# Pooling input and merge gates as seven half products, with their sums and other operands made in earlier stages

## The chip, the cores and the metric

The kernel runs on one core of one Trainium2 chip. The metric is device time in microseconds (us). A core has a matrix engine (TensorE, called PE in the profile), a vector engine (VectorE, DVE), an activation engine (ScalarE, ACT), a general engine (GpSimd, POOL) and a sync engine (SyncE, SP) that here only issues transfers. Each engine works through its own queue of instructions in order and waits on semaphores for the others. Matrices are read by PE from on-chip memory (SBUF), and its results stand in eight PSUM banks of 128 x 512 float32.

## The reference

One layer of an encoder, for 1024 tokens of width 1024, float32 throughout:

```python
h = rmsnorm(x, norm_mix)
q, k, v, r, lr_f, lr_b, u, g_a, g_b = split(h @ w_in)    # widths 512 512 1024 1024 16 16 512 1024 1024
o = gla(q, k, v, decay(lr_f)) + flip(gla(flip ..., decay(lr_b)))   # 4 heads, forward and backward scan
o = per_head_rmsnorm(o) * gla_norm * silu(r)
y_a = o @ w_branch_gla
pooled = window_mean(u, 2 / 4 / 8 / 16 per channel group) - u
y_b = (pooled @ w_pool_group) * pool_scale
x = x + (sigmoid(g_a) * y_a + sigmoid(g_b) * y_b) @ w_out
gate, up = split(rmsnorm(x, norm_ffn) @ w_ffn_in)         # 2 x 2816 columns
x = x + (silu(gate) * up) @ w_ffn_out
out = rmsnorm(x, norm_final)
```

What the change touches is the projection of h to u, g_a and g_b (2560 of the columns of w_in), and where the operands of `y_a` and of the product with w_out are prepared.

## The kernel before

Every operand of a large product is split into two float32r parts: `hi` is the value cast, `lo` the value less `hi`. A product a b is made of three matmuls, hi hi, hi lo and lo hi (`products`, L250); `mm3` issues the three for one 128 x 128 block of the left side and 512 columns of the right. `split_to` (L172 and L173) makes the parts: a cast on ScalarE, then a subtraction on POOL for weights and mostly on DVE for the rest.

*Seven products for eight.* In the branch product, the merged product and both FFN products, left and right matrix are cut into 2 x 2 blocks and the result is made of seven block products of sums and differences (numbered 1 to 7 in the code) instead of eight (a Strassen-Winograd scheme). Such a product of blocks is called a half product. Such sums are extra vector work. All projections out of `w_in` (q, k, v, r, u, g_a, g_b) are done plainly.

*Weights.* `load` (L180) issues transfers from SP into a ring of four raw buffers; `order` lists which columns of `w_in` come when; `take` hands out the next weights and `prepare` puts the split of the ones after them into the list `pending`. `pump`, called after each `mm3`, releases one pending split each time two `mm3` of 512 columns have been issued.

*Work beside.* The order on each engine is written out by hand, without a scheduler. Vector work that accompanies matmuls is written as generators. `begin` puts one in the list `side`, and `pump` resumes the first of them when as many `mm3` have been issued as its last `yield` said. `finish_side` runs them out at once. `attention` (L450 on) is such a generator: decay factors, the backward scan, the scores, the forward scan, for one head, beside the projections of the next head. In the scan each step (`advance`) goes from PE (`kv`) to DVE (`st`, L539) to ScalarE (`sf`, L615) and back to PE (`op`, L616).

*Stages*, by the time in the trace: normalization and transposes, with v of head 0 and the low-rank decay (to about 74 us); q, k, v of heads 1 to 3 with the attention of the head before beside each (74 to 284); r with the rest of the last attention, where o is transposed and multiplied by silu(r) into `oT` (284 to 394, L655 to L675); the gate stage (394 to 633, L948 to L995); the branch product (633 to 709); the merged product with w_out (709 to 794); the FFN-in product, 22 `Unit`s of seven products (794 to 1225); the FFN-out product (1225 to 1451).

*The gate stage before.* For each of the four groups g there is one 128-column block of u, and two blocks each of g_a and g_b, each block being 2 halves x 8 `mm3`. u goes through `pooled` (a generator: running window sums on DVE), its result stays in SBUF and is multiplied with the group's weights into `yb`; the gates go through a sigmoid, g_b's is multiplied by yb, and both go to DRAM (`sa_out`, `yb_out`). After each half, `beside` (L941) resumes one step of preparations for later stages: `branch_sums` (sums of blocks of w_branch on POOL, L753), `output_parts` (sums of blocks of w_out on POOL, L778, then their split, all stored to `wo_out`), `unit_parts` (the operands of the first two FFN units, stored to `u_out`). `later` notes a store, and `flush` (L685 to L690) issues those noted, on ScalarE's queue. `early` makes three sets of sums of oT for the branch product at the end of the stage (L865, L867, L870).

SBUF is used in 39 slots of 512 KB (128 partitions x 1024 float32) beside smaller rings.

```python
    def later(dst, src):
        deferred.append(partial(nc.scalar.dma_start, dst, src))
...
            for half in range(2):
                ps = feature_major(wa, hT, half)
                nc.scalar.activation(sa[:, half, :], ps[:, :], AF.Sigmoid)
                beside(j)
            flush()
            later(sa_out[:, :, j, :], sa[:, :, :])
```

Of the kernel before, what the change touches and what calls it, by code (L numbers as in the profile page):

```python
# [42 lines left out]
AHEAD = 4  # L43

# [5 lines left out]
def kernel(  # L50
# [91 lines left out]
    side = []  # L142
# [3 lines left out]
    def pump(dt):  # L146
        if pending:
            credit[0] += dt
            if credit[0] >= 2:
                credit[0] = 0.0  # L150
                pending.pop(0)()
        if not side:
            return
        side[0][1] -= dt
        while side and side[0][1] <= 0:
            try:
                side[0][1] += next(side[0][0])
            except StopIteration:
                side.pop(0)
# [55 lines left out]
    for g in range(GROUPS):  # L215
        order.append((w_in, KT, U0 + g * P, P))
        for j in (2 * g, 2 * g + 1):
            order.append((w_in, KT, GA0 + j * P, P))
            if j == 2 * g:
                order.append((w_pool_group[0, g], 1, 0, 2 * P))  # L220
            order.append((w_in, KT, GB0 + j * P, P))
# [214 lines left out]

    v_heads, o_heads, unscaled = {}, {}, []
# [11 lines left out]
    def attention(h, q, k):  # L449
# [181 lines left out]
        o_heads[h] = o  # L631

        def normalize():
            for n in range(NT):
                t = o[n // 4][:, n % 4, :]
                nc.vector.tensor_scalar(t, t, rs[:, n : n + 1], None, op0=ALU.mult)

# [3 lines left out]

    for h in range(HEADS):
# [11 lines left out]
    oT = {}  # L654
    for j in range(KT):  # L655
        if j == 6:
            finish_side()
        if j % 4 == 0:
            for half in range(2):
                oT[j // 4, half] = [slot(s="o") for _ in range(2)]  # L660
        w = take()
        for half in range(2):
# [4 lines left out]
            for i in range(4):  # L667
# [5 lines left out]
                oT[j // 4, half][j % 4 // 2][:, j % 2, :], tp[:, :], g_gla[:, j : j + 1], sr[:, :],  # L673
                op0=ALU.mult, op1=ALU.mult,
            )  # L675


    sa_out, yb_out = (dram.tile([P, 2, KT, HALF], F32, name=n) for n in ("sa_out", "yb_out"))
    deferred = []

    def later(dst, src):
        deferred.append(partial(nc.scalar.dma_start, dst, src))

    def flush():
        while deferred:  # L685
            deferred.pop(0)()

# [28 lines left out]

    add = partial(nc.vector.tensor_tensor, op=ALU.add)
    sub = partial(nc.vector.tensor_tensor, op=ALU.subtract)
    psub = partial(nc.gpsimd.tensor_tensor, op=ALU.subtract)
    padd = partial(nc.gpsimd.tensor_tensor, op=ALU.add)

    s_out = {p: dram.tile([P, 4, HALF], F32, name=f"s_out{p}") for p in (3, 5, 6, 7)}
    wo_out = {p: dram.tile([2, P, 4, HALF], F32, name=f"wo_out{p}") for p in range(1, 8)}
    READY = 2
    f_order = [f for q in range(PAIRS) for f in (q, q + PAIRS)]
    u_out = [{p: dram.tile([P, 2, HALF], F32, name=f"u_out{n}_{p}") for p in range(1, 8)} for n in range(READY)]

    def chunk(w, k_half, c_half, c):
        k0 = (4 * k_half + 2 * c) * P
        return w[k0 : k0 + 2 * P, c_half * HALF : (c_half + 1) * HALF].rearrange("(k p) c -> p k c", p=P)  # L740

    def branch_sums(c):
        raw = {}
        for i in range(2):
            for j in range(2):
                raw[i, j] = slot(s="wsum")
                nc.sync.dma_start(raw[i, j][:, :, :], chunk(w_branch, j, i, c))
        yield
        x11, x12, x21, x22 = (raw[i, j][:, :, :] for i in range(2) for j in range(2))
        for op, dst, a, b, p in (  # L750
            (padd, x22, x21, x22, 5), (psub, x21, x11, x21, 7), (psub, x11, x22, x11, 6), (psub, x12, x12, x11, 3)
        ):
            op(dst, a, b)  # L753
            later(s_out[p][:, 2 * c : 2 * c + 2, :], dst)
            if p in (7, 3):
                yield
        yield

    def output_parts(c):
        raw = {}  # L760
        for i in range(2):
            for j in range(2):
                raw[i, j] = slot(s="wsum")
                nc.sync.dma_start(raw[i, j][:, :, :], chunk(w_out, i, j, c))
        yield
        b11, b12, b21, b22 = (raw[i, j][:, :, :] for i in range(2) for j in range(2))

        def parts(p, src):
            hi, lo = slot(F32R, s="wph"), slot(F32R, s="wpl")
            split_to(hi[:, :, :], lo[:, :, :], src)  # L770
            for n, t in enumerate((hi, lo)):
                later(wo_out[p][n][:, 2 * c : 2 * c + 2, :], as_f32(t[:, :, :]))

        for p, src, dst, a, b in (
            (1, b11, b11, b12, b11), (3, b22, b12, b22, b12), (7, b12, b22, b22, b11), (2, b21, b21, b21, b22)
        ):
            parts(p, src)
            psub(dst, a, b)  # L778
            if p in (3, 2):
                yield  # L780
        for p, src in ((5, b11), (6, b22), (4, b21)):
            parts(p, src)
            if p != 5:
                yield
        yield

    def unit_parts(n):
        raw = []
        for c0 in (f_order[n] * P, D_FF + f_order[n] * P):
            raw.append(slot(F32, (KT, P), "fraw"))  # L790
            nc.sync.dma_start(raw[-1][:, :, :], w_ffn_in[:, c0 : c0 + P].rearrange("(k p) c -> p k c", p=P))
        yield
        a11, a12, a21, a22 = (t[:, 4 * j : 4 * j + 4, :].rearrange("p k c -> p (k c)") for t in raw for j in range(2))

        def parts(p, src):
            both = slot(F32R, s="up")
            split_to(both[:, 0, :], both[:, 1, :], src)
            later(u_out[n][p][:, :, :], as_f32(both[:, :, :]))

        parts(1, a11)  # L800
        parts(4, a22)
        padd(a22, a21, a22)
        psub(a21, a11, a21)
        yield
        parts(2, a12)
        parts(5, a22)
        psub(a11, a22, a11)
        psub(a12, a12, a11)
        yield
        for p, src in ((7, a21), (6, a11), (3, a12)):  # L810
            parts(p, src)
        yield
        yield
# [43 lines left out]
    ob = {(i, j): oT[i, 1 - j] for i in range(2) for j in range(2)}  # L857
    t2s = []
    begun = {}

    def branch_sum(p, c):

        b11, b12, b21, b22 = (ob[i, j][c][:, :, :] for i in range(2) for j in range(2))
        if p == 5:
            sub(b11, b12, b11)  # L865
        elif p == 7:
            sub(b12, b22, b12)  # L867
        elif p == 6:
            t2s.append(slot(s="t2"))
# [4 lines left out]
    def branch_piece(p, c):  # L874
# [6 lines left out]
        def sums():  # L881
            if p == 4:
                branch_sum(4, c)

        def make(raw):
            b = {1: ob[0, 0], 2: ob[1, 0], 3: ob[1, 1], 4: ob[1, 0], 5: ob[0, 0], 6: t2s, 7: ob[0, 1]}[p][c]
            return weight_split(raw), begun.pop((p, c), None) or data_split(b)
# [46 lines left out]
    preps = [g for c in range(2) for g in (branch_sums(c),)] + [output_parts(c) for c in range(2)]  # L934
    preps = chain(*preps, *(unit_parts(n) for n in range(READY)))

    def begin_first(c):
        begun[1, c] = data_split(ob[0, 0][c])

    early = [partial(begin_first, c) for c in range(2)]  # L940
    early += [partial(branch_sum, p, c) for p in (5, 7, 6) for c in range(2)]  # L941

    def beside(j):
        next(preps, None)
        if j == KT - 1:
            for _ in range(2):
                early.pop(0)()

    for g in range(GROUPS):
        w = take()  # L950
        u = [t2(HALF + 2 * PAD, s="u") for _ in range(2)]
        nc.gpsimd.memset(u[0][:, :PAD], 0.0)
        nc.gpsimd.memset(u[1][:, PAD + HALF :], 0.0)
        for half in range(2):
            ps = feature_major(w, hT, half)
            nc.scalar.copy(u[half][:, PAD : PAD + HALF], ps[:, :])
        pool = slot(F32R, s="ph"), slot(F32R, s="pl")
        begin(pooled(g, u, *pool), 1)
        for j in (2 * g, 2 * g + 1):
            c = slice((j % 2) * P, (j % 2 + 1) * P)  # L960
            wa = take()
            if j == 2 * g:
                wp = take()(0)
            sa = slot(s="sa")
            for half in range(2):
                ps = feature_major(wa, hT, half)
                nc.scalar.activation(sa[:, half, :], ps[:, :], AF.Sigmoid)
                beside(j)
            flush()
# [659 lines left out]
```

## Time and profile before

| what | before |
| --- | --- |
| median of 3 runs | 1452.88 us (1450.63 to 1453.42) |
| the profiled execution's own time | 1452.8 us |
| its span in the profile | 1451.1 us |
| mean granted clock of TensorE | 0.995 |
| PE busy | 1405.5 us, 97%, 6797 instructions |
| DVE busy | 872.5 us, 60% |
| POOL busy | 743.8 us, 51% |
| ACT busy | 561.8 us, 39% |
| moved by DMA | 234.15 MB |

The span runs from the first to the last instruction in the profile, and the execution's own time is 1.7 us longer. A row of the table by stage gives the window and its length, then busy time and count of instructions of each engine, the granted clock, the share of time in which the 16 DMA engines are busy, and GB/s. A row of the timeline gives the start, the duration, the engine, the line of the kernel, the operation and its tiles, and in brackets how long the engine stood idle before it and what released it. A row of the groups gives the line, engine, operation and shapes with the count, then busy time in us with the mean in ns, then the idle time before and what ended it. Matmuls overlap in the pipeline, so a matmul's own duration is longer than the distance to the next.

### The profile page before, as it was taken

The page shows a single profiled execution, that of the slowest core. Times are in us where ns is not written, and L with a number is a line of the kernel's source. Part 1 is how long each engine was busy: PE and PEld are TensorE (multiplying, and loading weights), DVE is VectorE, ACT ScalarE, POOL GpSimd, SP SyncE. Part 2 cuts the span into 40 slices and gives each one's busy share as a digit, 9 for nine tenths or more (in the row PEclk, how much of TensorE's full clock was granted, in tenths as well). Part 3 has the DMA queues.
Part 4 walks back from the last instruction along what each step waited for, and adds up shares of the span by engine and source line. Part 5 has one row for each costly group of instructions (what it writes and reads, how often), then busy time and mean ns, then how long its engine had stood idle before and what let it go on. Part 6 is the DMA issues. An engine that isn't in the chain of part 4 may idle for free. (4 is left out here: it accounts for less than half of the span.)

```text
span 1451.1 us, 18652 instructions
## 1 busy us (share of the span) xinstructions
PE 1405.5 (97%) x6797; PEld 1179.6 (81%) x6797; DVE 872.5 (60%) x1111; ACT 561.8 (39%) x995; POOL 743.8 (51%) x510
## 2 busy tenths in 40 slices
PE   7999999999999999999999989999999999999988
PEld 6889898888888787888777778888888888778876
DVE  6266767662132463477994777777677777465375
ACT  6364655652122333344125523322323323444243
POOL 3240413222264553456743457666666668597355
PEclk9999999999999999999999999999999999999999
DMA  6120201011176768686666556444544446966362
GB/s 186 44 58 2 59 16 44 15 30 37 50 224 206 274 214 293 236 290 252 191 203 225 182 178 195 152 154 160 163 153 152 151 154 222 351 234 255 131 240 79
DMA packets 164732, 234.15 MB, mean 161 GB/s; under 512 B 10873, under 2 KB 97953, under 8 KB 164641
## 3 DMA queue, kind: packets, MB, share of 16 engines
q1 hardware_dynamic: 151936, 194.17, 40.7%
q10 hardware_dynamic: 12704, 38.80, 7.1%
q8 instruction: 53, 0.87, 0.2%
q14 instruction: 39, 0.31, 0.1%
HBM read 158.22 MB, written 74.71 MB: 161 GB/s over the span
## 5 line engine op out<-in xcount | busy, mean ns | idle before, releaser
L173 POOL TENSOR_TENSOR wl<-raw,wh 128x512 fp32r<-128x512 f32 (+1 forms) x91 | 124.6, 1387 | 257.3 <-ACT wh L172 212.4
L250 PE MATMUL ps<-gh,wl 128*128 128x512 f32 x616 | 240.8, 391 | 4.0 <-POOL wl L173 4.0
L250 PE MATMUL ps<-gh,wh 128*128 128x512 f32 x616 | 240.9, 391 | 0.1
L250 PE MATMUL ps<-gl,wh 128*128 128x512 f32 x616 | 240.2, 390 | 0.0
L250 PE MATMUL ps<-hh,wh 128*128 128x512 f32 x576 | 229.3, 398 | 5.2 <-ACT wh L172 5.2
L250 PE MATMUL ps<-hh,wl 128*128 128x512 f32 x576 | 226.1, 393 | 1.2 <-POOL wl L173 1.2
L250 PE MATMUL ps<-hl,wh 128*128 128x512 f32 x576 | 225.4, 391 | 0.0
L173 POOL TENSOR_TENSOR wl<-fs,wh 128x512 fp32r<-128x512 f32 x80 | 112.4, 1405 | 97.9 <-ACT wh L172 69.7
L250 PEld LDWEIGHTS ps<-gh,wl 128*128 128x128 f32 x616 | 116.0, 188 | 29.2 <-POOL wl L173 4.8
L172 ACT CAST wh<-fs 128x512 fp32r<-128x512 f32 x80 | 49.8, 622 | 230.2 <-DVE fs L1101 221.4
L250 PEld LDWEIGHTS ps<-gh,wh 128*128 128x128 f32 x616 | 116.1, 189 | 24.3 <-issue 0.5
L250 PEld LDWEIGHTS ps<-gl,wh 128*128 128x128 f32 x616 | 115.9, 188 | 23.8
L173 POOL TENSOR_TENSOR ol<-gor,oh 128x1024 fp32r<-128x1024 f32 (+1 forms) x42 | 109.2, 2617 | 47.0 <-ACT oh L172 46.1
L250 PEld LDWEIGHTS ps<-hh,wh 128*128 128x128 f32 x576 | 108.9, 189 | 27.0 <-ACT wh L172 6.0
L250 PEld LDWEIGHTS ps<-hh,wl 128*128 128x128 f32 x576 | 108.9, 189 | 25.3 <-POOL wl L173 2.1
L250 PEld LDWEIGHTS ps<-hl,wh 128*128 128x128 f32 x576 | 109.1, 189 | 21.3
L250 PE MATMUL ps<-oh,ol 128*128 128x512 f32 x308 | 120.2, 390 | 4.9 <-POOL ol L173 4.9
L250 PE MATMUL ps<-ol,oh 128*128 128x512 f32 x308 | 120.0, 389 | 2.9 <-DVE ol L173 2.9
L250 PE MATMUL ps<-oh,oh 128*128 128x512 f32 x308 | 120.0, 390 | 0.0
L173 DVE TENSOR_TENSOR ol<-wor,oh 128x1024 fp32r<-128x1024 f32 (+1 forms) x42 | 87.6, 2112 | 39.0 <-ACT oh L172 30.2
L173 POOL TENSOR_TENSOR wl<-fraw,wh 128x512 fp32r<-128x512 f32 x60 | 94.3, 1571 | 16.3 <-ACT wh L172 16.3
L250 PE MATMUL ps<-wh,hh 128*128 128x256 f32 x256 | 79.7, 311 | 0.0
(255 smaller groups left out, 2878.3 us busy)
## 6 DMA issues: line engine op xcount, KB each, us to landing
raw<-in_w_in_dram SPq DMA_DIRECT2D x88, 256.0 KB, 3.1
fraw<-in_w_ffn_in_dram SPq DMA_DIRECT2D x44, 512.0 KB, 5.6
gor<-g_out SPq DMA_DIRECT2D x35, 512.0 KB, 5.4
g_out<-s SPq DMA_DIRECT2D x44, 256.0 KB, 2.4
wor<-t_out SPq DMA_DIRECT2D x20, 512.0 KB, 8.2
g_out<-g SPq DMA_DIRECT2D x33, 256.0 KB, 3.4
x<-in_x_dram SPq DMA_DIRECT2D x16, 512.0 KB, 4.6
wor<-in_w_ffn_out_dram SPq DMA_DIRECT2D x15, 512.0 KB, 7.4
```

Of the source, the lines that this page charges most:

```text
L172: nc.scalar.copy(hi, src)
L173: eng.tensor_tensor(lo, src, as_f32(hi), op=ALU.subtract)
L250: nc.tensor.matmul(ps, a[i], b[j], start=first and n == 0, stop=last and n == 2)
```

## The change

The 20 column blocks of u, g_a and g_b become ten units of two blocks, each made of seven products: two units for u, then eight of (g_a, g_b) blocks. `Unit`, which served the FFN alone, moves up and takes its matrix, columns and order of products; a new class `Gates` puts the seven results together (a copy on ScalarE and seven additions on DVE) and applies sigmoid and yb. The right side's sums come from hT: `feature_jobs` restores hi + lo, takes differences and splits them, beside r from j = 3.

The preparations of w_branch and w_out (`branch_jobs`, `output_jobs`) are cut into pieces of 128 x 512 and run beside the attention, from head 1's projections to the start of r, through a second list, `aside`, that `pump` steps too (every 2.9 `mm3`; the features every 2.3). In `beside`, a job passes through operation, cast, subtraction and store, one step at a time. The first FFN units' operands (`unit_jobs`) start with the sixth gate unit counted from zero. All stores noted by `later` go to SP's queue. o of heads 0 to 2 goes to DRAM (`o_out`) and is loaded during r; oT goes to DRAM (`ob_out`) and is loaded at the end of the gate stage; the pooling results go through `p_out`, and the w_pool_group weights are loaded by `load_pooled`. After `prepare` the credit starts at -2, so that a split begins two `mm3` later. Of the early sums of oT none is left in the gate stage: `branch_sum` makes them inside the branch product (for products 6, 7 and 4). The attention is run out before j = 3 of r instead of j = 6.

```diff
+    def flush(eng=nc.sync):
+        while deferred:
+            eng.dma_start(*deferred.pop(0))
...
     def pump(dt):
...
+        if aside:
+            aside[0][1] -= dt
+            if aside[0][1] <= 0:
+                cost = next(aside[0][0], None)
+                if cost is None:
+                    aside.pop(0)
+                else:
+                    aside[0][1] += cost
...
             ready.append(Weights(loaded.pop(0)))
+
+            credit[0] = -2.0
...
+    def branch_jobs(k):
+        (x11, x12, x21, x22), loads = rows_of(w_branch, k, True)
+        yield from loads
+        for op, dst, a, b, p in (
+            (padd, x22, x21, x22, 5), (psub, x21, x11, x21, 7), (psub, x11, x22, x11, 6), (psub, x12, x12, x11, 3)
+        ):
+            yield partial(op, dst, a, b), None, s_out[p][:, k, :]
+
+    def output_jobs(k):
+        (b11, b12, b21, b22), loads = rows_of(w_out, k)
+        yield from loads
+        for op, p, src in (
+            (None, 1, b11), (None, 3, b22), (None, 2, b21), (partial(psub, b11, b12, b11), 5, b11),
+            (partial(psub, b12, b22, b12), 7, b12), (partial(psub, b22, b22, b11), 6, b22),
+            (partial(psub, b21, b21, b22), 4, b21),
+        ):
+            yield op, src, wo_out[p][:, :, k, :].rearrange("n p c -> p n c")
...
+    def feature_jobs(c):
+        def restored(i, j):
+            hi, lo = (as_f32(t[:, :, :]) for t in hT.pair(2 * i + c, j))
+            whole = slot(s="hs")[:, :, :]
+            return whole, (partial(add, whole, hi, lo), None, None)
...
+    def beside(jobs, every, put):
...
+            for pair in puts.pop(0):
+                nc.sync.dma_start(*pair)
...
+                nc.vector.tensor_tensor(lo, src, as_f32(hi), op=ALU.subtract)
...
+                nc.scalar.copy(parts[0], src)
...
+            yield every
...
+        if h == 0:
+            prepare_beside([*map(branch_jobs, range(4)), *map(output_jobs, range(4))], 2.9)
...
+    load_o(0)
     for j in range(KT):
+        if j == 3:
+            finish_side()
+            finish_beside()
+            prepare_beside([feature_jobs(0), feature_jobs(1)], 2.3)
+        if j in (1, 3):
+            load_o(j // 2 + 1)
+        w = take()
         if j == 6:
-            finish_side()
...
+            next_gate_unit()
...
+        if j % 2:
+            flush()
+            for half in range(2):
+                c = j % 4 // 2
+                later(ob_out[j // 4, half][:, 2 * c : 2 * c + 2, :], oT[half][:, :, :])
+    finish_beside()
...
     def branch_sum(p, c):
...
-        if p == 5:
-            sub(b11, b12, b11)
-        elif p == 7:
+        if p == 7:
             sub(b12, b22, b12)
         elif p == 6:
+
+            sub(b11, b12, b11)
             t2s.append(slot(s="t2"))
             sub(t2s[c][:, :, :], b22, b11)
...
         def sums():
-            if p == 4:
-                branch_sum(4, c)
+            if p in (6, 7, 4):
+                branch_sum(p, c)
...
+    gate_units = [(U0 + 2 * i * P, U0 + (2 * i + 1) * P) for i in range(2)]
+    gate_units += [(GA0 + j * P, GB0 + j * P) for j in range(KT)]
+    GATES = (1, 6, 2, 7, 5, 4, 3)
...
+        def run(self, p):
+            ps = bank(next(mm_banks))
+            product(self.unit, p, ps, right)
+            ps = ps[:, :]
+            x0, x1, y0, y1 = (t[:, half, :] for t in self.rows for half in range(2))
+            done = None
+            if p == 1:
+                nc.scalar.copy(x0, ps)
+            elif p == 6:
+                add(x1, ps, x0)
...
+            elif p == 5:
+                add(y1, ps, y0)
+                add(x1, ps, x1)
+                done = y1
...
+            if done is not None and self.n >= 2:
+                nc.scalar.activation(done, done, AF.Sigmoid)
...
+    for n in range(len(gate_units)):
+        z = Gates(n)
+        last = n == len(gate_units) - 1
+        if n == 6:
             finish_side()
...
+            prepare_beside(map(unit_jobs, range(READY)), 4, 1)
...
+        if n >= 2 and n % 2 == 0:
+            load_pooled(n // 2 - 1)
+        for at, p in enumerate(GATES):
+            if coming:
+                gunits[coming.pop(0)[0]].step()
+            elif at == 5:
                 line_make()
+            z.run(p)
+            if at == 0:
+                flush()
+            if at == 1:
+                next_gate_unit()
...
+            if last and at == 1:
+                load_block(0, 0)
...
+        if n < 2:
+            begin(pooling(z.rows, 2 * n), 2)
+        else:
+            z.store()
```

More of the change, by code (lines that the diff above doesn't have):

```diff
@@ new lines, in loading, with loads, rows_of @@
+    def loading(srcs, tiles):
+        def loads():
+            for t, src in zip(tiles, srcs):
+                nc.sync.dma_start(t, src)
+        yield loads, None, None
+        for _ in range(2):
+            yield None, None, None
+    def rows_of(w, k, left=False):
+        raw = [slot(s="wsum") for _ in range(2)]
+        both = w[:, :].rearrange("(i k p) (j c) -> k p i j c", i=2, p=P, j=2)[k]
+        x11, x12, x21, x22 = (t[:, i, :] for t in raw for i in range(2))
+        srcs = [both[:, :, i, :] if left else both[:, i, :, :] for i in range(2)]
+        return (x11, x12, x21, x22), loading(srcs, [t[:, :, :] for t in raw])
@@ L736 @@
[L736 to L813, printed above, removed]
@@ L1324, in run @@
             self.banks[p] = bank(next(mm_banks))
-            product(self.unit, p, self.banks[p])
+            product(self.unit, p, self.banks[p], split_b)
             ps = self.banks[p][:, :]
```

379 lines of the change are left out of this document (244 added, 135 removed).

## The prediction

> **What bounds the kernel now.** I read, in this order: the busy times of the page, the chain that ended last, a table of busy time by stage, then 4 us windows and the timeline where a stage is longer than its matmuls need.
>
> ```profile
> span 1451.1 us, 18652 instructions
> PE 1405.5 (97%) x6797; PEld 1179.6 (81%) x6797; DVE 872.5 (60%) x1111; ACT 561.8 (39%) x995; POOL 743.8 (51%) x510
> ```
> ```profile
> 862.35 360.35 PE ps L250 x1582
> ```
> ```profile
> core 0: us, PE busy (x) PEld busy (x) DVE busy (x) ACT busy (x) POOL busy (x), PEclk, DMA share, GB/s
> 74.00:148.00 74.00, 73.52 (x469) 66.66 (x468) 47.80 (x95) 44.12 (x96) 21.92 (x15) 1.00 0.11 29
> 148.00:217.00 69.00, 68.53 (x449) 62.73 (x448) 49.05 (x101) 40.10 (x89) 20.22 (x15) 1.00 0.14 38
> 217.00:284.00 67.00, 65.46 (x435) 59.29 (x434) 45.65 (x96) 37.32 (x85) 18.14 (x13) 1.00 0.11 29
> 284.00:394.00 110.00, 106.67 (x551) 89.54 (x550) 42.29 (x81) 36.61 (x76) 26.80 (x21) 1.00 0.14 35
> 394.00:633.00 239.00, 232.59 (x1009) 190.98 (x1008) 99.80 (x102) 74.56 (x124) 114.57 (x74) 0.99 0.71 240
> 633.00:709.00 76.00, 75.89 (x335) 62.54 (x334) 58.05 (x52) 31.47 (x45) 58.08 (x37) 1.00 0.72 258
> 862.00:1222.00 360.00, 359.65 (x1580) 297.68 (x1581) 253.53 (x278) 108.58 (x188) 257.45 (x177) 1.00 0.50 166
> ```
>
> TensorE is busy 97% of the span, so a matmul taken away is worth its pitch if vector work and transfers keep up. The chain's piece of 1582 matmuls in 360.35 us gives that pitch: 0.2278 us. (A row's own 0.39 us overlaps the next.) The stages are: heads 1, 2 and 3 with their attention beside them (74 to 148, 217, 284), r and the transposes of o (to 394), pooling and gates (to 633), the branch product (to 709), later the merged product and the FFN. The gate stage's 1009 matmuls need 1009 x 0.2278 = 229.8 us and it takes 239: 9.2 us are lost. The windows show where.
>
> ```profile
> 494.00:498.00 4.00, 1.94 (x9) 1.28 (x7) 0.00 (x0) 0.00 (x0) 0.00 (x0) 1.00 1.03 408
> 498.00:502.00 4.00, 2.69 (x7) 1.86 (x8) 1.38 (x1) 3.07 (x5) 2.52 (x2) 0.78 0.91 264
> 502.00:506.00 4.00, 4.00 (x15) 3.21 (x15) 0.31 (x1) 1.14 (x2) 2.55 (x2) 0.79 1.03 385
> ...
> 546.00:550.00 4.00, 1.71 (x8) 1.09 (x6) 0.00 (x0) 0.55 (x2) 0.00 (x0) 1.00 1.02 391
> 550.00:554.00 4.00, 3.26 (x8) 2.34 (x9) 2.70 (x3) 2.51 (x5) 2.52 (x2) 0.68 1.00 263
> ```
> ```profile
> 496.83 1.15 ACTq L686 DMA_DIRECT2D wo_out<-wpl  x1
> 498.02 0.62 ACT L172 CAST wh<-raw 128x512 fp32r<-128x512 f32 x1 [8.60 <-issue]
> ...
> 498.69 0.50 PE L250 MATMUL ps<-hh,wh 128*128 128x512 f32 x1 [2.75 <-ACT wh L172]
> ...
> 500.46 0.63 PE L250 MATMUL ps<-hh,wh 128*128 128x512 f32 x1
> ...
> 500.88 0.63 PE L250 MATMUL ps<-hl,wh 128*128 128x512 f32 x1
> ```
>
> Two stalls. ScalarE computes nothing for 8.60 us while its queue issues stores of the w_out operands at over a microsecond each, with the DMA engines full (share 1.03, 408 GB/s). The cast of the next weights stands behind them, and PE waits 2.75 us for it. Then matmuls come every 0.42 us (500.46 to 500.88) with a granted clock of 0.78 until about 503.8. The second stall (546 to 554) has the same form. The Trainium skill (TensorE: Matmul & The Clock Gate, "HAM oscillation — how this bites in real kernels") names PE gaps above about 3.4 us as what lowers the clock; here a shorter gap was followed by half pitch, so the measurement decides, and any new stall is priced with its slow tail.
>
> **The change, part by part.** The sum is made against the profiled execution's own 1452.8 us (span 1451.1 plus 1.7 around it), 0.1 below the median of the runs, 1452.88.
>
> (a) Fewer matmuls. Twenty 128-column blocks x 2 halves x 8 k x 3 matmuls = 960 matmuls become 10 units x 7 products x 4 k x 3 = 840. -120 x 0.2278 = **-27.3**.
>
> (b) The stores of the w_out operands leave the gate stage and ScalarE's queue. The two stalls go with them: **-9.2**. What is late next is costed under (e).
>
> (c) Beside the attention (heads 1 to 3 and the start of r) now stand the sums of w_branch and w_out on POOL, and the split of the w_out operands. Work of before, moved:
>
> ```profile
> L753 POOL TENSOR_TENSOR wsum<-wsum,wsum 128x1024 f32<-128x1024 f32 x8 | 20.2, 2520 | 0.3
> ...
> L778 POOL TENSOR_TENSOR wsum<-wsum,wsum 128x1024 f32<-128x1024 f32 x8 | 23.3, 2915 | 25.2 <-DVE wpl L173 18.6 <-issue 6.4
> ...
> L173 DVE TENSOR_TENSOR wpl<-wsum,wph 128x1024 fp32r<-128x1024 f32 x14 | 24.6, 1783 | 12.5 <-ACT wph L172 12.3
> ...
> L172 ACT CAST wph<-wsum 128x1024 fp32r<-128x1024 f32 x14 | 14.2, 1044 | 4.9 <-POOL wsum L778 4.7 <-DMA wsum<-in_w_out_dram 0.3
> ```
> ```profile
> 131.71 0.48 DVE L539 SCALAR_TENSOR_TENSOR st<-kv,fac,so 128x256 f32<-128x256 f32 x1 [1.07 <-PE kv L250]
> ...
> 132.29 0.51 ACT L615 ACTIVATE sf<-st,fac 128x256 f32<-128x256 f32 x1 [1.14 <-DVE st L539]
> ...
> 133.73 0.59 PE L616 MATMUL op<-sf,qe 128*128 128x256 f32 x2
> ```
>
> They become pieces of half that size: 32 sums of 43.5/32 = 1.36 us, 28 subtractions of 24.6/28 = 0.88, 28 casts of 0.51. By the order of instructions some 11, 13 and 8 sums fall in heads 1, 2 and 3, and about 8 and 13 of the subtractions in heads 2 and 3. As totals they fit: head 3's DVE would be 45.65 + 13 x 0.88 = 57 of 67 us, 85%. What can be late is the scan, a chain kv (PE), st (DVE), sf (ACT), op (PE) at each step. Here sf is ready at 132.29 + 0.51 = 132.80 and read at 133.73: 0.93 us of slack. A subtraction of 0.88 and a cast of 0.51 ahead in both queues exceed it by 0.46. Of the 21 subtractions in heads 2 and 3 about half meet a scan step: 10 x 0.46 = 5. POOL sums that slow the scan's DVE steps: 3, my choice. Bounds: 0, since nothing overruns its engine, and 43.5, every POOL sum holding DVE for its whole length on the path. I take **+8**, near the lower end: DVE and POOL stand at 70 and 72% in 862 to 1222 with PE at its pitch.
>
> The 28 stores, the loads of w_branch and w_out and the stores of o go to SP's queue.
>
> ```profile
> SPq L180 <- POOL wl L173: 437.5, 70, 40.8
> ```
>
> SP spends 437.5 us waiting there for a weight buffer, up to 40.8 at once, and a store queued behind it keeps its slot that long. Slots are then free late for the next sums, which have no user before the branch product (633): nothing. DMA traffic is light here (share 0.11 to 0.14).
>
> (d) r. DVE gets the sums of the features from j = 3 on: 16 sums and 8 subtractions of 128x1024. Rows of the same size, and of the gates' pieces for (e):
>
> ```profile
> L1101 DVE TENSOR_TENSOR fs<-fraw 128x512 f32<-128x512 f32 x20 | 24.2, 1208 | 0.0
> ...
> L173 POOL TENSOR_TENSOR wl<-fraw,wh 128x512 fp32r<-128x512 f32 x60 | 94.3, 1571 | 16.3 <-ACT wh L172 16.3
> ...
> L1336 DVE TENSOR_TENSOR p<-ps,p 128x512 f32<-128x512 f32 x19 | 13.0, 684 | 12.3 <-PE ps L250 12.3
> ...
> L979 DVE SCALAR_TENSOR_TENSOR sb<-yb,cols,sb 128x512 f32<-128x512 f32 x16 | 12.0, 749 | 69.2 <-PE yb L250 56.6 <-ACT sb L976 12.6
> ...
> 621.24 2.35 DVE L865 TENSOR_TENSOR o<-o,o 128x1024 f32<-128x1024 f32 x2
> 627.80 4.36 DVE L867 TENSOR_TENSOR o<-o,o 128x1024 f32<-128x1024 f32 x2
> ...
> gate<-sa_out SPq DMA_DIRECT2D x8, 512.0 KB, 5.3
> ```
>
> The two L865 pieces took 1.18 us each, the two L867 pieces 2.18. 24 x 1.18 is 28 us, 24 x 2.18 is 52; on top of 42.29 of 110 us there is room, most of it behind j = 3 where the attention has ended: nothing, and if that cover were gone, the part of 52 us that overruns. But o of head 0 now comes back from DRAM: its load is issued just before r's first 24 matmuls (5.5 us), takes about 5.3 us once issued (the gate row) and stands behind stores. Bounds 0 and one load's landing; **+2**.
>
> (e) Gates. Per unit DVE makes 4 sums (at most 4 x 1.208), 7 evacuations (7 x 0.684) and 2 products with the scale (2 x 0.749): 11.1 us at most for 84 + 6 matmuls, 20.5 us. With the pooling chain beside units 2 to 4, unit 2 holds some 33 DVE instructions by the order, at 0.684 22.6 us: over its 20.5. Pooling results now go out to DRAM and come back before the unit that uses them; where they are late, the pooling is run out at once ahead of that unit's matmuls, on DVE. POOL's 7 subtractions (7 x 1.571 = 11.0 us) and ScalarE's casts fit. Weights arrive as two tiles of 512 KB, issued after the second product of the unit before, in the same queue as the stores of the unit before that, and behind any wait of theirs: 4 x 5.3 = 21 us if one by one, against the 5 products left (60 matmuls, 13.7 us) and four operands made ahead; they run side by side (408 GB/s at 494 against 512 KB in 5.3 us, 99 GB/s, for one), so this is close and not surely late. Bounds 0 and 11 (the two stalls again and the 2 us by which unit 2 overruns); **+4**, between them.
>
> (f) Branch product. The b sums of products 6 and 7 move in: 2.35 + 4.36 = 6.7 us of DVE work (L865, L867), DVE standing at 58 of 76, and o comes back in 4 MB. Bounds 0 and 6.7; **+3**. Merged product: its stores of x change from ScalarE's queue to SP's, among the loads; 0, with 2 either way.
>
> Sum: -27.3 - 9.2 + 8 + 2 + 4 + 3 = -19.5, so 1433.3.
>
> **The rivals.** *Everything is hidden*: only (a) and (b) count, -36.5: 1416. For it: every stage has idle DVE, ACT and POOL; against it: the scan's 0.93 us of slack is less than one subtraction and one cast.
>
> *Slower: POOL's sums lock DVE during the scan.* Each 1.36 us sum holds a scan step of DVE beyond its 0.93 us of slack, and PE stops behind it; at the worst, every sum on the path, +43.5 in (c) for +8: 1452.8 - 36.5 + 43.5 + 9 = 1469. It decides from 27.5 us lost in the heads, that is 36.5 less the 9 of (d) to (f). For it: one DVE sum took 1.18 us at 621 and 2.18 at 627. Against it: 862 to 1222 again. The Trainium skill (SBUF — State Buffer, "Who interferes with whom") has DVE and GpSimd share one port pair as an exclusive lock, the loser blocked; the 1.18 against 2.18 agrees, 70 plus 72% busy at full pitch bounds what it costs.
>
> *The stall only changes queue*: loads of gate weights late behind stores on SP. Each costs half of 9.2, 4.6 us with its slow tail; four of them in place of +4: -36.5 + 18.4 + 8 + 2 + 3 = -5, 1448; five make no change. For it: 408 GB/s was the ceiling at 494; against it: the w_out stores that filled the DMA engines there have left the stage.
>
> **How the numbers follow.** My sum's case, 1424 to 1442: 0.47. All hidden, 1410 to 1424: 0.20. Stalls on SP, 1442 to 1456: 0.18. The lock, above 1456: 0.15. The range 1410 to 1458 leaves out most of the last. A change of 0.2% (2.9 us) is about what can be told from none: 1449.9 to 1455.7 counts as the same. Faster takes the first two and half of the third, 0.76; the same 0.06; slower the lock and a little of the third, 0.18.
>
> **What would show it.** (a), (b): a gate stage of 840 + 48 matmuls in 202 to 207 us, the clock at 1.00 throughout and no cast behind a store. (c): heads longer by 2 to 4 us each, PE waiting for sf or kv behind DVE's and ACT's wo pieces; over 9 us each would be the lock, with DVE's scan steps above 0.48. (d): a wait of PE for the load of o at r's start. (e): waits for wl or wh at the head of units. (f): PE waiting for DVE's sums in the branch product. The prediction is wrong if PE's losses lie in stages that I hold at nothing, the FFN above all, whose code only moves.

## The result and the profile after

The changed kernel takes 1464.99 us (median of 4 runs, 1462.99 to 1469.0), the kernel before, run beside it, 1453.15: a ratio of 1.0086, 95% interval 1.0059 to 1.0112. It is 12 us slower; 1433 was forecast, with a range up to 1458. The profiled execution took 1464.93 us. From the page of the changed kernel:

```profile
span 1463.1 us, 18944 instructions
PE 1391.6 (95%) x6677; PEld 1162.3 (79%) x6677; DVE 983.9 (67%) x1263; ACT 594.3 (41%) x1057; POOL 784.0 (54%) x552
```

PE has 120 instructions fewer, as (a) said; DVE is busy 111 us longer. The busy times by stage tell where the time went. The three stretches are: from the first decay matmul of head 0 to the last transpose of r; from there to the first matmul of the branch product; the branch product. First before, then after:

```profile
74.67:393.29 318.62, 312.80 (x1891) 276.99 (x1890) 184.79 (x371) 157.16 (x343) 87.09 (x62) 1.00 0.13 33
393.29:632.98 239.69, 233.28 (x1013) 191.63 (x1012) 99.80 (x102) 75.05 (x124) 114.57 (x74) 0.99 0.71 239
632.98:709.54 76.56, 76.45 (x337) 62.99 (x336) 58.59 (x53) 31.49 (x45) 58.34 (x38) 1.00 0.72 256
```
```profile
72.95:417.27 344.32, 321.46 (x1890) 282.83 (x1889) 250.66 (x425) 179.64 (x379) 136.38 (x92) 0.98 0.41 135
417.27:632.61 215.34, 207.30 (x893) 167.21 (x892) 140.02 (x193) 83.92 (x147) 105.28 (x86) 0.99 0.55 183
632.61:720.26 87.65, 80.58 (x337) 64.70 (x336) 69.19 (x61) 32.80 (x47) 59.38 (x39) 0.96 0.73 272
```

| stretch | before | after | change | forecast |
| --- | --- | --- | --- | --- |
| up to the first decay matmul | 74.67 | 72.95 | -1.7 | 0 |
| heads 1 to 3 and r | 318.62 | 344.32 | +25.7 | +10, (c) and (d) |
| gates | 239.69 | 215.34 | -24.4 | -32.5, (a), (b) and (e) |
| branch product | 76.56 | 87.65 | +11.1 | +3, (f) |
| merged product | 84.65 | 83.90 | -0.8 | 0 |
| FFN to the end of the span | 656.91 | 658.94 | +2.0 | 0 |

In the heads and in the branch product the count of PE instructions is the same, and DVE has 65.9 and 10.6 us more to do. In three places the loss is larger than forecast, by 15.7, 8.1 and 8.1 us: together the 32 us between forecast and result.

The 25.7 us of heads and r are of two kinds. PE stands still 17.0 us longer (22.86 us without a matmul for 5.82), and the same matmuls keep it busy 8.7 us longer (321.46 for 312.80), with a mean granted clock of 0.98 for 1.00. In the list of PE's waits in this stretch, those for `kt` and for what `kt` is made from (`ke`, `fac`) grow from 3.6 to 16.0 us, those for the scores `p` from 0.4 to 4.6; `sf` of the scan, which (c) priced, does not appear.

The longest new wait stands in the decay factors of a head, not in its scan. The timeline of the changed kernel, and below it the same place before:

```profile
224.77 1.24 DVE L675 TENSOR_TENSOR fac<-fac 128x4 f32<-128x4 f32 x1
225.94 2.38 DVE L569 TENSOR_TENSOR up<-wsum,up 128x512 fp32r<-128x512 f32 x2
228.24 0.67 DVE L644 TENSOR_TENSOR la<-la,z 128x512 f32<-128x512 f32 x1
...
229.53 2.06 POOL L584 TENSOR_TENSOR wsum<-wsum 128x512 f32<-128x512 f32 x1
231.12 1.02 DVE L673 TENSOR_TENSOR ke<-ke,k 128x512 f32<-128x512 f32 x1
231.56 1.71 POOL L674 TENSOR_TENSOR qe<-qe,q 128x512 f32<-128x512 f32 x1
232.06 1.22 DVE L675 TENSOR_TENSOR fac<-fac 128x4 f32<-128x4 f32 x1
232.31 0.62 ACT L578 CAST up<-wsum 128x512 fp32r<-128x512 f32 x1
233.31 0.60 ACT L181 CAST kt<-kp 128x512 fp32r<-128x512 f32 x1
233.96 0.58 PE L254 MATMUL kv<-vh,kt 128*128 128x256 f32 x1 [4.95 <-ACT kt L181]
```
```profile
218.15 0.15 DVE L509 TENSOR_TENSOR fac<-fac 128x4 f32<-128x4 f32 x1
218.22 0.67 DVE L478 TENSOR_TENSOR la<-la,z 128x512 f32<-128x512 f32 x1
...
221.43 0.68 DVE L507 TENSOR_TENSOR ke<-ke,k 128x512 f32<-128x512 f32 x1
222.03 0.15 DVE L509 TENSOR_TENSOR fac<-fac 128x4 f32<-128x4 f32 x1
223.75 0.39 PE L250 MATMUL kv<-vh,kt 128*128 128x256 f32 x1 [0.87 <-ACT kt L172]
...
289.42 0.39 PE L250 MATMUL kv<-vh,kt 128*128 128x256 f32 x1 [1.21 <-ACT kt L172]
```

PE already waited here before the change, 0.87 and 1.21 us: this chain, DVE for the most part, ended just too late with no added work at all. Now it ends some 4 us later (4.95, and 3.74 in the next head). Two things lengthen it: pieces of the w_out operands (`up`) between its steps, and steps that run beside a POOL instruction. From the start of one `fac` to the start of the next `la` it took 0.07 us before and takes 3.5 now, 2.3 of it for two subtractions of w_out operands; a cast of them (232.31) stands ahead of the cast of `kt` as well. The product of four elements per partition (`fac`) shows the second by itself: 0.15 us alone, 1.22 beside POOL, here beside the attention's own `qe`, which the sums had pushed back in POOL's queue.

### The profile page after: what moved, and what is told of

Its sections match the earlier page's. It is cut to its first block, busy times and chain, and to the rows that moved or that the text cites. A ratio compares the mean times of both kernels' runs of the same rounds, so it can differ in the third digit from the quotient of the medians.

```text
span 1463.1 us, 18944 instructions
## 1 busy us (share of the span) xinstructions
PE 1391.6 (95%) x6677; PEld 1162.3 (79%) x6677; DVE 983.9 (67%) x1263; ACT 594.3 (41%) x1057; POOL 784.0 (54%) x552
## 5 line engine op out<-in xcount | busy, mean ns | idle before, releaser
L182 POOL TENSOR_TENSOR wl<-fs,wh 128x512 fp32r<-128x512 f32 x120 | 164.4, 1372 | 178.9 <-ACT wh L181 140.0
L181 ACT CAST wh<-fs 128x512 fp32r<-128x512 f32 x120 | 74.2, 621 | 306.4 <-DVE fs L848 294.3
L182 POOL TENSOR_TENSOR wl<-fraw,wh 128x512 fp32r<-128x512 f32 x90 | 135.5, 1505 | 49.2 <-ACT wh L181 49.1
L254 PE MATMUL ps<-hh,wh 128*128 128x512 f32 x376 | 152.3, 405 | 1.8 <-DVE ga L1156 1.2
L254 PE MATMUL ps<-hh,wl 128*128 128x512 f32 x376 | 148.6, 395 | 1.0 <-POOL wl L182 1.0
L254 PE MATMUL ps<-hl,wh 128*128 128x512 f32 x376 | 148.4, 395 | 0.0
L182 POOL TENSOR_TENSOR wl<-raw,wh 128x512 fp32r<-128x512 f32 x47 | 68.8, 1476 | 148.5 <-ACT wh L181 140.0
L254 PEld LDWEIGHTS ps<-hh,wh 128*128 128x128 f32 x376 | 71.8, 191 | 17.4 <-issue 2.4
L254 PEld LDWEIGHTS ps<-hh,wl 128*128 128x128 f32 x376 | 71.7, 191 | 17.4 <-POOL wl L182 1.8
L254 PEld LDWEIGHTS ps<-hl,wh 128*128 128x128 f32 x376 | 71.8, 191 | 13.4
```

Source lines behind the costliest of these rows:

```text
L181: nc.scalar.copy(hi, src)
L182: eng.tensor_tensor(lo, src, as_f32(hi), op=ALU.subtract)
L254: nc.tensor.matmul(ps, a[i], b[j], start=first and n == 0, stop=last and n == 2)
```

## The experiments

**What lengthens the heads: POOL's sums, the splits, or the transfers.** Three kernels leave work out beside the attention. `e1_no_sums`:

```diff
-            (None, 1, b11), (None, 3, b22), (None, 2, b21), (partial(psub, b11, b12, b11), 5, b11),
-            (partial(psub, b12, b22, b12), 7, b12), (partial(psub, b22, b22, b11), 6, b22),
-            (partial(psub, b21, b21, b22), 4, b21),
+            (None, 1, b11), (None, 3, b22), (None, 2, b21), (None, 5, b11),
+            (None, 7, b12), (None, 6, b22), (None, 4, b21),
...
-            yield partial(op, dst, a, b), None, s_out[p][:, k, :]
+            yield partial(lambda *args: None, dst, a, b), None, s_out[p][:, k, :]
```

> Leaves out the 32 sums of w_branch and w_out on POOL beside the attention (the pieces are stored and split as loaded, so later products use other data); loads, stores, casts and DVE subtractions stay. The changed kernel took 344.3 us from the first decay matmul of head 0 to the end of r, the kernel before 318.6: 25.7 more. Theory A (POOL's sums hold DVE): that stretch falls to 318-327 and the time to about 1441-1449. Theory B (the w_out casts and subtractions stand in ACT's and DVE's queues ahead of the attention's own work): it stays at 337 or more, the time at 1457 or more. Theory C (transfers, the SP queue or the later weight splits): no change.

`e2_no_split`:

```diff
-            yield op, src, wo_out[p][:, :, k, :].rearrange("n p c -> p n c")
+            yield op, None, [(wo_out[p][n, :, k, :], src) for n in range(2)]
...
+                elif isinstance(dst, list):
+                    puts[0] += dst
```

> Leaves out the 28 casts on ACT and 28 subtractions on DVE of the w_out operands beside the attention (the unsplit pieces are stored twice, same bytes); POOL's sums stay. Theory A: from the first decay matmul to the end of r still 335 us or more. Theory B: 318-327 us, the time about 1441-1449. Theory C: no change.

`e3_no_ops` has both edits.

> Leaves out both, the POOL sums and the w_out splits beside the attention; loads and stores stay. Theories A and B: the stretch is back at 318-323 us, the time about 1440. Theory C: it stays above 335. In between: the rest above 319 is what transfers, o through DRAM and the later weight splits cost.

They took 1454.17, 1454.78 and 1447.68 us, one execution each. The heads and r, in this order:

```profile
73.17:409.74 336.57, 318.65 (x1891) 280.76 (x1890) 240.24 (x425) 179.33 (x379) 88.64 (x60) 0.98 0.43 138
```
```profile
74.28:410.92 336.64, 317.71 (x1891) 280.46 (x1890) 230.44 (x397) 165.19 (x351) 133.03 (x92) 0.98 0.43 138
```
```profile
74.52:398.81 324.29, 314.58 (x1890) 278.25 (x1889) 222.46 (x397) 165.46 (x351) 86.34 (x60) 0.99 0.44 143
```

From 344.3, each alone takes off 7.7 us, both together 20.0, and neither theory A nor B holds by itself. (Seven profiled kernels with the same work beside the heads took 342.7 to 344.3 us here, so 7.7 is clear of the spread.) In e2 one wait of 7.71 us from 237 us on, with DVE idle, comes from its own bunched stores: SP issues six of them in a row, and the next weights come late. Its gain is understated by about that much, so that the 20.0 doesn't show that sums and splits reinforce each other. Both take DVE's time: without the sums DVE is busy 10.4 us less (they slow it), without the splits 20.2 less. 5.7 of the 25.7 us remain with no such work: transfers, o through DRAM and the features' sums in r; these weren't told apart.

At the two longest waits, though, the two can be told apart. First e1, then e2, at the places where the changed kernel waits 4.95 and 3.74 us:

```profile
230.64 0.58 PE L254 MATMUL kv<-vh,kt 128*128 128x256 f32 x1 [4.58 <-ACT kt L181]
303.53 0.58 PE L254 MATMUL kv<-vh,kt 128*128 128x256 f32 x1 [3.80 <-ACT kt L181]
```
```profile
228.53 0.39 PE L254 MATMUL kv<-vh,kt 128*128 128x256 f32 x1 [0.99 <-ACT kt L181]
313.35 0.39 PE L254 MATMUL kv<-vh,kt 128*128 128x256 f32 x1 [2.06 <-ACT kt L181]
```

Without the sums these waits stay; without the splits they are much nearer to their size before the change (0.87 and 1.21). What the sums cost lies in other, shorter waits and in the pace of the matmuls: in e1 PE stands still 17.9 us for the changed kernel's 22.9, and is busy 318.7 for 321.5.

**Does the place matter?** `e4_hold` keeps the added work out of the decay factors, `e7_early` starts it sooner and thins it out, `e9_stretch`, built on the slower pooling of e8 below, gives the decay factors more matmuls to hide behind.

```diff
-        if aside:
+        if aside and not held[0]:
...
+        held[0] = True
         decay(1, 1)
...
+        held[0] = False
         while h not in v_heads:
...
-            prepare_beside([*map(branch_jobs, range(4)), *map(output_jobs, range(4))], 2.9)
+            prepare_beside([*map(branch_jobs, range(4)), *map(output_jobs, range(4))], 2.2)
```

> The same work beside the attention, but its list is held while a head's first three decay factors and its keys are made (about 18 of 64 products per head), and goes every 2.2 products for 2.9 elsewhere. If the place decides (the gaps of 4.95 and 3.74 us, and the slow matmuls after them, stand in that phase): the stretch falls from 344 to 322-330 us, the time to 1443-1451. If only the amount of work counts, wherever it stands: 340 or more, the time 1460 or more.

```diff
+        if h == 0:
+            prepare_beside(map(branch_jobs, range(4)), 1.3)
+            prepare_beside(map(output_jobs, range(4)), 4.6)
         qk = project_qk()
```

> The sums of w_branch start 32 products earlier, beside q and k of head 0 where the vector engines are nearly idle, every 1.3 products; the w_out operands follow, every 4.6 instead of 2.9. If it is the density of added vector work beside the decay factors: from the first decay matmul to the end of r falls from 344 to 326-335 us, the time to 1446-1456. If any such piece in a decay phase costs the same: 340 or more.

```diff
         decay(1, 1)
-        yield 3.5
+        yield 4.0
...
-        yield 4.2
+        yield 5.2
...
-        yield 5.0
+        yield 6.5
         kts = {(1, 1): transposed_keys(1, 1)}
-        yield 5.0
+        yield 7.0
```

> Beside the slower pooling, five more products of 64 per head are allowed between the steps of the decay factors and the first scan (4, 5.2, 6.5 and 7 for 3.5, 4.2, 5 and 5); no work is added or left out. If the chain of decay factors on DVE, without slack already before the change, turns every added piece into a wait of PE: from the first decay matmul to the end of r falls from 344 to 330-338 us, the time from 1455.6 to 1441-1450. If DVE's total or the scan steps bound the heads: 342 or more, 1454 or more.

Measured: 1463.15, 1479.21 and 1463.14 us; heads and r in the three kernels:

```profile
74.48:415.50 341.02, 321.05 (x1891) 282.73 (x1890) 248.76 (x425) 180.13 (x379) 133.37 (x92) 0.97 0.42 138
```
```profile
75.70:430.54 354.84, 323.93 (x1891) 284.05 (x1889) 249.37 (x425) 179.53 (x378) 125.29 (x85) 0.97 0.38 126
```
```profile
73.12:423.46 350.34, 323.55 (x1890) 284.77 (x1889) 251.03 (x425) 183.94 (x382) 137.10 (x92) 0.97 0.40 133
```

In all three the second of the two cases came out; e9 is 7.5 us slower than the e8 that it is built on. Holding the work shortened the two waits (2.23 for 4.95, 0.26 for 3.74) and opened others (1.29 for a later `kt`, 1.15 and 2.61 before the scores, 3.04 for the load of o). Stretching made new waits, for `kt` behind DVE (2.58 and 3.52) and for weights from POOL (1.56, 1.71). Starting early held up the weights of head 1 (3.93 us for a cast). My theory that only the place is wrong falls: each move only moved the waits. But the amount of DVE time alone doesn't set the length either: DVE is busy 249 to 251 us in all three, as in the changed kernel, and the stretch takes 341.0 to 354.8.

**POOL's lock, or DVE's time?** `e13_dve_sums` has DVE make the 32 sums, on a base with slower pooling and stores on ACT's queue (e8 and e11 below), which takes 1449.7 us with 344.1 in heads and r.

```diff
-            (padd, x22, x21, x22, 5), (psub, x21, x11, x21, 7), (psub, x11, x22, x11, 6), (psub, x12, x12, x11, 3)
+            (add, x22, x21, x22, 5), (sub, x21, x11, x21, 7), (sub, x11, x22, x11, 6), (sub, x12, x12, x11, 3)
```

> On the version with slower pooling and stores on ACT's queue (1449.7 us, heads and r 344.1): the 32 sums of w_branch and w_out are made by DVE instead of POOL; nothing is left out. A sum of this size takes DVE 0.68 us alone, 22 us in all. If a sum on POOL costs because it locks DVE out (the 4-element product of the decay factors takes 0.15 or 1.24 us) : heads and r fall to 330-341 us, the time to 1437-1447. If DVE's own time is what lacks: 346 or more, 1452 or more.

It took 1457.53 us. Heads and r, and the `fac` instruction (duration in ns: least, median, longest) in this kernel, then that instruction in the changed one and in e1:

```profile
74.46:425.09 350.63, 325.85 (x1890) 286.08 (x1889) 261.54 (x457) 179.56 (x379) 90.21 (x60) 0.97 0.40 130
L675 DVE TENSOR_TENSOR fac<-fac x16: 150/156/1248, 91.7 to 332.7; 128x4 f32<-128x4 f32 x16
```
```profile
L675 DVE TENSOR_TENSOR fac<-fac x16: 148/1218/1251, 89.1 to 323.3; 128x4 f32<-128x4 f32 x16
```
```profile
L674 DVE TENSOR_TENSOR fac<-fac x16: 149/154/1292, 89.2 to 317.4; 128x4 f32<-128x4 f32 x16
```

With the sums off POOL the median `fac` is back at 0.156 us, so the lock is real. Yet the heads got 6.5 us longer, not shorter. A sum takes less of DVE's time by blocking it from POOL than by running on it: the 32 sums on POOL lengthen DVE's busy time by 10.4 us (the changed kernel less e1), and moving them to DVE adds another 10.1 (261.54 for 251.40 on this base). This fits that DVE's time is what lacks in the heads; that it is the whole price isn't shown, since e4, e7 and e9 differ at equal DVE time. The Trainium skill (SBUF — State Buffer, "Who interferes with whom") says that a DVE instruction with two SBUF inputs contends with a GpSimd one that reads SBUF, and calls their shared ports an exclusive lock. The two values of `fac` agree.

**The gate stage.** `e5_no_pool` leaves out the window sums; `e8_slow_pool` spreads them:

```diff
-                yield 1.5 * cost
+                yield (3 if g else 1.5) * cost
```

> Leaves out the window sums of the pooling chain in the gate stage (u is split as it is); everything else stays. The gate stage took 215.3 us, 13 more than its 888 matmuls at 0.2278 (202.3); most of the gaps lie at 470 to 520 us, in units 2 and 3. If DVE, overrun by pooling beside the units' own sums and evacuations, makes them: the stage falls to 204-208 us and the time by 7 to 11. If weights come late behind stores on SP: it stays at 213 or more.

> The pooling chain of groups 1 to 3 goes at half the pace, up to unit 6. If DVE's overrun in units 2 and 3 makes the gate stage's gaps: the stage falls from 215.3 to 205-210 us, the time by 5 to 10, to 1455-1460. If weights are late: no change.

e5 took 1450.57 us (one execution), e8 1455.63 (ratio to before 1.0022, 1.0008 to 1.0036). The changed kernel at the longest wait of the stage, then the stage in e5 and in e8:

```profile
478.39 0.69 DVE L946 TENSOR_TENSOR ws<-u 128x527 f32<-128x527 f32 x1
479.12 0.71 DVE L952 TENSOR_TENSOR ws<-ws 128x525 f32<-128x525 f32 x1
479.74 0.68 DVE L1158 TENSOR_TENSOR ga<-ps,ga 128x512 f32<-128x512 f32 x1
480.34 0.68 DVE L1159 TENSOR_TENSOR ga<-ps,ga 128x512 f32<-128x512 f32 x1
481.17 0.75 DVE L1178 SCALAR_TENSOR_TENSOR ga<-yb,cols,ga 128x512 f32<-128x512 f32 x1
481.98 0.79 PE L254 MATMUL ps<-trh,wh 128*128 128x512 f32 x1 [2.79 <-DVE ga L1178]
```
```profile
415.89:620.43 204.54, 203.04 (x894) 166.89 (x892) 114.15 (x157) 83.76 (x147) 104.89 (x86) 1.00 0.59 192
```
```profile
419.01:624.82 205.81, 203.10 (x893) 166.93 (x892) 137.42 (x193) 84.06 (x147) 106.83 (x86) 1.00 0.59 191
```

PE waits for a bank that DVE empties late, because pooling (`ws`) stands in the same queue. With pooling at half pace the stage falls from 215.3 to 205.8 us with no work left out: 9.5 us, as expected of DVE's overrun.

Three more stand on e8. `e11_act_stores` returns the stores that `later` notes to ACT's queue; `e12_no_credit` and `e15_act_no_credit` drop the line `credit[0] = -2.0`, without and with that.

```diff
-    def flush(eng=nc.sync):
+    def flush(eng=nc.scalar):
```

> With the slower pooling; all noted stores go to ACT's queue again, as before the change. If SP's queue held up loads or slots: faster than 1455.6 by 2 or more. If stores held ACT's casts back as at 496 us before the change: slower by 4.6 per such stall, 1460-1475. If neither: within 2 us.

> With the slower pooling; a weight split begins at once instead of two products later, as before the change. If the later split takes part in the heads' loss: the stretch to the end of r falls by 2 or more from 344 us. If not: within 2 us, 1454-1458 in all.

> The same version, with the weight splits begun at once. If the 1.5 us seen between the two earlier runs is real: 1447-1449; if it is noise: 1449-1451.

e11: 1449.73 us, ratio to before 0.9979 (0.9965 to 0.9992). Its gate stage and branch product:

```profile
419.20:621.86 202.66, 202.58 (x893) 167.09 (x892) 138.55 (x194) 84.76 (x147) 107.87 (x87) 1.00 0.60 199
621.86:706.79 84.93, 78.92 (x337) 63.82 (x336) 67.71 (x60) 32.80 (x47) 60.26 (x38) 0.98 0.74 279
```

The stage is down to its matmuls (202.3): SP's queue had cost 3.1 us here. (In this stage the four kernels with the slower pooling and stores on SP, e8 among them, take 205.6 to 207.0; the four with stores on ACT take 202.3 to 203.2.) For the branch product nothing of the kind can be told: 84.9 in e11 and 87.6 in e8, but 84.8 in e9 with stores on SP and 87.0 in e14 with stores on ACT. In all, the change of queue took off 5.9 us here and 2.9 from e12 to e15. The casts that waited behind stores before the change don't wait here, though the stores of the gates are back in their queue, while those of the w_out operands go through SP beside the attention: this points at the w_out stores as what made those stalls. The credit took 1.5 us off once (1454.16 against 1455.63) and added 1.5 once (1451.26 against 1449.73): nothing that can be told.

**The branch product.** `e6_no_b_sums` leaves out all sums for half products 6 and 7; `e10_loads` issues the loads of o one product earlier, on top of e9.

```diff
-            sub(b21, b21, t2s[c][:, :, :])
+            sub(b21, b21, b22)
...
-            if p in (6, 7, 4):
+            if p == 4:
                 branch_sum(p, c)
...
```

> Leaves out the sums of the attention output for half products 6 and 7 that the change moved into the branch product (other blocks are used in their place); splits, loads and the late sum stay. The branch product took 87.65 us, before 76.56. If these sums on DVE make the loss: 77-81 us. If the reload of o from DRAM does: 84 or more.

```diff
-            if last and at == 1:
+            if last and at == 0:
                 load_block(0, 0)
...
-            elif last and at == 2:
+            elif last and at == 1:
                 line_load()
```

> As the stretched one, and the loads of the attention output and of the first branch weights are issued one product (2.7 us) earlier in the last gate unit. If the reload of o is late at the head of the branch product (two waits of 0.9 and 1.7 us): the branch falls by 2 to 4 us, to 84-86. If DVE is late with the split whenever the data comes: no change, 87-88.

The changed kernel where the product loses most, and the product in e6:

```profile
655.21 2.31 DVE L1027 TENSOR_TENSOR ob<-ob,ob 128x1024 f32<-128x1024 f32 x1
657.55 2.20 DVE L1029 TENSOR_TENSOR t<-ob,ob 128x1024 f32<-128x1024 f32 x1
...
662.01 0.68 DVE L1275 TENSOR_TENSOR mg<-ps,sum 128x512 f32<-128x512 f32 x1
...
669.27 2.18 POOL L1277 TENSOR_TENSOR mg<-mg,gate 128x512 f32<-128x512 f32 x1 [0.63 <-DVE mg L1276]
671.41 9.50 POOL L182 TENSOR_TENSOR wl<-wraw,wh 128x512 fp32r<-128x512 f32 x6
673.71 0.80 PE L254 MATMUL ps<-dh,wl 128*128 128x512 f32 x1 [2.83 <-POOL wl L182]
```
```profile
630.84:711.96 81.12, 77.56 (x337) 62.69 (x336) 61.47 (x55) 33.22 (x47) 59.91 (x39) 1.00 0.79 294
```

The sums delay DVE, so the merges (`mg`) come late; POOL's part of each merge waits for DVE with weight splits queued behind it, and PE waits 2.83 us for a split (`wl`). Without the sums the product takes 81.1 us (1456.95 in all, one execution), 6.5 less than the changed kernel. Two things weaken that figure. Kernels whose branch product has the same code (stores on SP) take 84.6 to 87.7 us for it, so the gain is 3.5 to 6.5. And e6 leaves out more than was moved: of its six sums the two of `t` stood inside the product before the change too:

```profile
633.92 4.46 DVE L870 TENSOR_TENSOR t<-o,o 128x1024 f32<-128x1024 f32 x2
```

e10 took 1463.1 us, with the branch at 86.9 against 84.8 in e9: no gain from loading earlier can be seen. 4.6 us, with waits for the first splits of o at the product's head, stay open.

**A version that beats both.** e11 does, by 0.2%. `e14_hold_act` joins it with the hold of e4.

> The same version, with the work beside the attention held during the decay factors (as in the earlier hold run, which took 3.3 us off heads and r): if the parts add up, heads and r 340-342 us, the time 1445-1448; if not, 1449 or more.

1448.75 us, ratio to before 0.9974 (0.9959 to 0.9989): the fastest median, 1.0 us below e11 and within its interval. Its heads and r took 343.6 us in the profile against e11's 344.1, which is within the spread, so the parts can't be shown to add up.

## Why the prediction was wrong

- (a) and (b) were right in mechanism and size. In e11, with nothing left out, the gate stage is 37.0 us shorter than before; -27.3 and -9.2 make 36.5. Only the two together were measured.
- (c) is the step that failed: "What can be late is the scan". I took the 0.93 us of slack of a forward scan step for the tightest place, and priced a piece by how far it overran it. The tightest place was the chain of decay factors, where PE already waited 0.87 and 1.21 us: slack below zero, so that added DVE time there lands on PE. The waits for `kt`, `ke` and `fac` went from 3.6 to 16.0 us, while PE has no wait for `sf`. The totals that I called fitting (85% of DVE in head 3) couldn't show this. (c) and (d) came to 25.7 us for 10, 20 of it from the added sums and splits. Of those, the splits make the two longest waits (e1, e2). 8.7 of the 25.7 are slower matmuls, which (c) priced at nothing.
- (d): no wait of PE for the load of o in the changed kernel, so that +2 was nothing; r lost 8.2 us to the last head's decay factors and scores instead.
- (e): the mechanism was named (unit 2 overruns DVE) and priced at 2 us of waits; it took 9.5 with the slow matmuls after it (e8), and SP's queue 3.1 more (e11). 13 us for 4, above the bound of 11.
- (f) was mis-sized: 11.1 us in the changed kernel, 8.0 at the least in kernels with the same branch code, for 3 with a bound of 6.7. The sums take part (3.5 to 6.5 us in e6, which leaves out two that hadn't moved); what makes the other 4.6 us stays open.
- The rivals: "everything is hidden" fell. The lock is there, but not as the price that I gave it: moving the sums from POOL to DVE made the heads longer (e13). The stall on SP's queue is right as a mechanism, at 3.1 us in the gate stage (e11) and without a stall like the one at 498 us.
- The argument that 862 to 1222 runs DVE at 70 and POOL at 72% with PE at its pitch didn't carry over. That a late piece has slack ahead of it there, and none in a chain from step to step, would explain it; no run tests this.

## What to carry to other kernels

Before hiding work under an engine's idle share, look for the waits that PE already has in that stage: a wait of 0.9 us says that the chain behind it has no slack, whatever the engine's mean says. Here the work moved to "idle" engines was paid most where it met a long dependent chain, and three modest moves onto one engine cost more than the matmuls that they saved. When such a change comes out slower, the pace of the side work and the queue of its stores are worth a run each: here they gave back 15 us with no change of the arithmetic.

## What the runs showed of the hardware

A DVE instruction of four elements per partition (`fac`) takes 0.15 us or about 1.24, by whether a POOL instruction runs at the same time: true of all 16 of them before the change (4 are long) and of all 16 after it (9 are long). It is the cheapest probe of the lock in this kernel. And PE's clock fell after shorter gaps than before the change, where the shortest of PE's waits ahead of such a fall was 2.41 us (PE starts again at 550.12). Windows of the changed kernel right after a gap of 1.56 us (PE starts again at 255.50), one of 1.97 (327.19) and one of 1.72 (641.40):

```profile
256.00:260.00 4.00, 3.78 (x18) 3.59 (x18) 3.94 (x7) 2.30 (x5) 3.44 (x3) 0.57 0.34 131
...
328.00:332.00 4.00, 4.00 (x14) 3.18 (x13) 2.73 (x5) 1.63 (x4) 0.00 (x0) 0.57 0.73 244
...
642.00:646.00 4.00, 4.00 (x19) 3.30 (x18) 4.00 (x3) 2.57 (x5) 4.00 (x3) 1.00 1.01 369
```

The granted clock (third number from the right) is 0.57 after the first two and 1.00 after the third, so the length of the gap alone doesn't decide it; what does wasn't tried. The mean clock fell from 0.995 to 0.988.
